# RWKV's transfers through DRAM for the blocks' inverses: part of them issued on ScalarE's queue instead of SyncE's

## The chip, the cores and the metric

The kernel runs on one core of a Trainium2 chip. A core has TensorE (PE) for products, VectorE (DVE), ScalarE (ACT) and GpSimd (POOL) for elementwise work, and SyncE (SP), which here only issues DMA transfers. Each engine works through its own instructions in order; between engines they wait for each other on counters (semaphores). A DMA can be issued from SyncE or from ScalarE; each has a queue of its own. The metric is the device time of one launch in microseconds (us), the median of several runs.

## What is computed

Two layers of a decoder with 256 positions and 1024 channels. In each layer three mixers (retention, forgetting attention and RWKV-7) work side by side on one input projection; their outputs are projected, weighted by gates, added, projected again and added to the input; then comes a SwiGLU feed-forward part. The change lies in RWKV-7, whose state is updated position by position:

```python
def _rwkv7_scan(r, w, k, v, a, b):
    def step(state, inp):
        r_t, w_t, k_t, v_t, a_t, b_t = inp
        sa = jnp.einsum('bhvk,bhk->bhv', state, a_t)
        state = (state * w_t[:, :, None, :] + sa[..., None] * b_t[:, :, None, :]
                 + v_t[..., None] * k_t[:, :, None, :])
        return state, jnp.einsum('bhvk,bhk->bhv', state, r_t)
...
    y = _rwkv7_scan(r_h, hd(decay), k_h, v_h, -kk, kk * a_h)
    y = _head_layernorm(y, RWKV_GN_EPS).reshape(B, S, RWKV_W) * gn_gain
...
    return (y + bonus.reshape(B, S, RWKV_W)) * g

def reference(x, ...):
    for l in range(DEPTH):
        h = _rmsnorm(x, mix_norm[l])
        proj = (h @ w_in[l]).astype(jnp.float32)
...
        merged = (gates[:, :, 0] * (y_ret.astype(x.dtype) @ p_ret[l])
                  + gates[:, :, 1] * (y_fox.astype(x.dtype) @ p_fox[l])
                  + gates[:, :, 2] * (y_rwkv.astype(x.dtype) @ p_rwkv[l]))
        x = x + merged @ w_out[l]
...
```

## The kernel before

**Weights and wide products.** Every product with a weight is done in three parts, high by high, high by low and low by high (L305, L308, L309), to keep float32 accuracy. A weight load of up to 1 MB goes to one of three buffers `raw` (L278, on SyncE's queue). ScalarE rounds a piece of 1024 columns to `whi` (L288), VectorE takes the rest to `wlo` (L289); there are four buffers of each. One piece serves 24 wide products of 128 by 128 by 256. The numbers behind the names (`whi_1935`) are the program's, in the order in which the text makes them.

**RWKV in chunks.** The 256 positions are cut into 4 chunks of 64. For each of the 4 heads and 4 chunks (16 units, handled as 8 pairs of heads) the kernel builds 64 by 64 matrices of the products inside a chunk (`gg`, L810) and needs the inverse of a triangular one. It inverts the four diagonal blocks of 16 by 16 directly and doubles the size twice by products: 16 to 32 (L888 and L895) and 32 to 64 (L907 and L915). The direct inversion is a recurrence of 15 steps on VectorE (L867 multiplies, L869 sums) with one block per partition, while in `gg` a block's rows lie on 16 partitions. So the blocks change their place through DRAM:

1. eight writes from `gg` to `d1` (L820), one for each half h of the partitions and each diagonal block b, 8 KB each;
2. two reads of `d1` to `lt` (L823), the same data for both halves of the columns; GpSimd then sets the diagonals to 1 (L824);
3. the recurrence from `lt` and the unit matrix to `ti`;
4. two writes of `ti` to `d2` (L873), 32 KB each;
5. eight reads of `d2` to the diagonal blocks of `tb` (L878), 8 KB each.

VectorE transposes the two halves of `tb` to `dn` (L883), and TensorE starts the doubling with L888. The results go on through L925 (`pu`), L936 (`par`), L948, L957 to the recurrence over chunks (L967, L972) and the output (L982), then squares (L988), a normalization on VectorE (L990, L394 to L401, L993) and a transposition on TensorE (L1000).

**What sets the order.** RWKV's steps and the wide products are written as generators that take turns by a table of numbers (PACE). What they emit is then put in order for each engine by a scheduler, which goes by priorities and by its own estimate of when each instruction could run. So an edit of the queue that a transfer is issued on can move other instructions too. Each transfer reports its end on one of eight counters (DMAHW0 to DMAHW7), which are taken in turn; a transfer whose counter still belongs to an unfinished one waits for that one first. RWKV's chain runs beside the gates and projections; the products of the third merge (L598 with its wide products) need its result.

Of the kernel before, what the change touches and what calls it, by code (L numbers as in the profile page):

```python
# [24 lines left out]
C = 64  # L25
NC = T // C
B = 32
Q = 16
# [129 lines left out]
class Kernel:  # L158
# [544 lines left out]
    def rwkv(self, l, rw):  # L703
        nc, c = self.nc, self.c
# [96 lines left out]
        gg = big.tile([P, NU, 3 * C], F32, name="gg")  # L801
# [13 lines left out]
        d1 = self.dr.tile([4, 2, NP, Q, Q], F32, name=f"d1_{l}")  # L815
        d2 = self.dr.tile([4, 2, NP, Q, Q], F32, name=f"d2_{l}")
        for h in range(2):
            for b in range(4):
                o = b * Q
                nc.sync.dma_start(d1[b, h].rearrange("u s t -> s u t"), gg[64 * h + o:64 * h + o + Q, h::2, 2 * C + o:2 * C + o + Q])  # L820
        lt = big.tile([P, Q, Q], F32, name="lt")
        for g4 in range(2):
            nc.sync.dma_start(lt[g4 * 64:(g4 + 1) * 64].rearrange("p s t -> p (s t)"), d1.rearrange("b h u s t -> (b h u) (s t)"))  # L823
        nc.gpsimd.memset(lt.rearrange("p s t -> p (s t)")[:, 0:Q * Q:Q + 1], 1.0)  # L824
        ti = big.tile([P, 8, Q], F32, name="ti")
        nc.sync.dma_start(ti, self.dc("tinit"))
# [1 line left out]
        tb = big.tile([P, NP, 2, C], F32, tag="q4", bufs=7, name=self.nm("tb"))  # L828
# [9 lines left out]
        for which in range(2):  # L838
            for a in range(2):
# [6 lines left out]
                else:  # L846
                    mean = sm.tile([P, 2 * NC], F32, tag="mean", bufs=2, name=self.nm("mean"))
                    nc.vector.tensor_reduce(out=mean, in_=ptr, axis=AX.X, op=ALU.add)
                    for h in range(2):
                        nc.scalar.copy(ma[hs[h], a * NC:(a + 1) * NC, C:], ptr[hs[h], h::2, :])  # L850
                        o = hs[1 - h]
# [5 lines left out]
        for p in range(NP):  # L857
            for h in range(2):
                o = hs[1 - h]
# [10 lines left out]
            if i % 6 == 0:  # L870
                yield PACE["rwkv11"]
        for g4 in range(2):
            nc.sync.dma_start(d2.rearrange("b h u c j -> (b h u) c j")[:, g4 * 8:(g4 + 1) * 8, :].rearrange("q c j -> q (c j)"),  # L873
                              ti[g4 * 64:(g4 + 1) * 64].rearrange("p c j -> p (c j)"))
        for h in range(2):
            for b in range(4):
                o = b * Q
                nc.sync.dma_start(tb[64 * h + o:64 * h + o + Q, :, h, o:o + Q], d2[b, h].rearrange("u c j -> c u j"))  # L878
        yield PACE["rwkv12"]

        dn = self.t2.tile([P, NP, C], F32, tag="t2", name=self.nm("dn"))
# [49 lines left out]
        for a in (1, 0):  # L931
            pa = self.ps.tile([P, NC - 1, 2 * C], F32, tag="sm", bufs=SM, name=self.nm("par"))
            for q in range(1, NC):
                for h in range(2):
                    u = unit(a, q, h)
# [8 lines left out]
        for q in range(NC - 1):  # L944
            for a in range(2):
                for h in range(2):
                    u = unit(a, q, h)
# [4 lines left out]
        for q2 in range(NC // 2):  # L952
            for a in range(2):
                for h in range(2):
                    for e in range(2):
                        u = unit(a, 2 * q2 + e, h)
# [19 lines left out]
        for q2 in (1, 0):  # L976
            for a in range(2):
                for e in (1, 0):
                    for h in range(2):
                        q = 2 * q2 + e  # L980
# [267 lines left out]
```

## Time and profile before

| | |
|---|---|
| time, median of 3 runs | 785.89 us (784.91 to 788.56) |
| the profiled execution | 787.26 us, its span 785.5 us |
| SyncE's queue (q1) | 28016 packets, 139.10 MB |
| HBM traffic | 136.97 MB read, 1.33 MB written |
| mean DMA rate | 179 GB/s |
| L888 in layer 0 and layer 1 | from 147.76 and 534.61 us |

Times in rows of the trace are microseconds from the start of the span. A row of the timeline gives the start, the duration, the engine, the line, the operation with output and input, and how often it is repeated; in brackets the idle time of the engine ahead of it and what ended it. "SPq" and "ACTq" are DMA issues of SyncE and ScalarE. Groups give busy time and the mean of one instruction. In the chain of waits each row is one stretch of the chain that ended last, followed back from the end. The ends of products are modelled, and products overlap, so their starts say more than their durations. Layer 0 takes roughly the first half of the span; the places of layer 1 lie 386 to 387 us behind those of layer 0.

### The profile page before, as it was taken

What the parts mean: (1) busy time and instruction counts of PE and PEld (TensorE: products, weight loads), DVE (VectorE), ACT (ScalarE), POOL (GpSimd) and SP (SyncE); (2) the same over time, 40 slices, a digit from 0 to 9 for tenths busy, and PEclk for the clock granted to TensorE, in tenths of its full rate; (3) what the DMA queues carried; (4) which work ended last, traced back from release to release, by engine and by line L of the source; (5) the groups of instructions that cost most, each with busy time, mean ns of one, the idle gap of its engine ahead of it and who ended that gap; (6) DMA issues with size and microseconds to landing.
All of it is one profiled execution on the core that took longest, in us unless ns stands there. A gap on an engine that the chain in (4) does not pass through costs nothing.

```text
span 785.5 us, 16513 instructions
## 1 busy us (share of the span) xinstructions
PE 774.2 (99%) x7002; PEld 754.9 (96%) x7002; DVE 569.7 (73%) x919; ACT 405.0 (52%) x563; POOL 17.8 (2%) x53
## 2 busy tenths in 40 slices
PE   8999999999999999999999999999999999999998
PEld 7999999989999999999998998998999999999997
DVE  5887989968867666656667798987788766666453
ACT  6577545345645454444446774544456544544331
POOL 3100000010000000000020000000000000000000
PEclk9999999999999999999999999999999999999999
DMA  8755434335655555456564554443255455555650
GB/s 325 259 175 183 156 121 164 136 103 198 222 184 195 193 184 214 158 192 201 202 204 178 175 175 162 126 159 138 96 221 194 167 210 204 176 210 172 206 186 28
DMA packets 28234, 140.42 MB, mean 179 GB/s; under 512 B 7648, under 2 KB 9216, under 8 KB 13184
## 3 DMA queue, kind: packets, MB, share of 16 engines
q1 hardware_dynamic: 28016, 139.10, 50.7%
q8 instruction: 55, 0.90, 0.5%
q10 hardware_dynamic: 144, 0.26, 0.1%
q14 instruction: 19, 0.16, 0.1%
HBM read 136.97 MB, written 1.33 MB: 176 GB/s over the span
## 4 chain that ended last, share of the span: by engine, by line
PE 91%; DVE 3%; DMA 2%; ACT 1%; SPq 1%; issue 1%; DVEq 0%; ACTq 0%
PE mm L309 26%; PE mm L305 26%; PE mm L308 26%; DVE wlo L289 1%; DMA d<-ti 1%; PE mqk L488 1%; PE mqk L487 1%; PE mqk L486 1%; DMA raw<-in_win 1%; ACT whi L288 1%; PE mv L488 1%; PE mv L486 1%; PE mv L487 1%; SPq L878 1%; PE pl L1103 1%
## 5 line engine op out<-in xcount | busy, mean ns | idle before, releaser
L288 ACT CAST whi<-raw 128x1024 fp32r<-128x1024 f32 (+1 forms) x257 | 264.8, 1034 | 302.4 <-PE mm L308 214.4
L289 DVE TENSOR_TENSOR wlo<-raw,whi 128x1024 fp32r<-128x1024 f32 (+1 forms) x257 | 308.6, 1203 | 140.0 <-ACT whi L288 139.1
L305 PE MATMUL mm<-xh,whi 128*128 128x256 f32 x1312 | 366.3, 279 | 1.3 <-ACT whi L288 0.9
L308 PE MATMUL mm<-xl,whi 128*128 128x256 f32 x1264 | 351.6, 278 | 0.3 <-DVE xl L442 0.3
L309 PE MATMUL mm<-xh,wlo 128*128 128x256 f32 x1264 | 351.3, 278 | 0.2 <-DVE wlo L289 0.2
L305 PEld LDWEIGHTS mm<-xh,whi 128*128 128x128 f32 x1312 | 246.8, 188 | 2.4 <-ACT whi L288 1.1
L308 PEld LDWEIGHTS mm<-xl,whi 128*128 128x128 f32 x1264 | 237.5, 188 | 1.2 <-issue 0.5
L309 PEld LDWEIGHTS mm<-xh,wlo 128*128 128x128 f32 x1264 | 237.3, 188 | 1.2 <-issue 0.5
L309 PE MATMUL mm<-hi,wlo 128*128 128x256 f32 x576 | 159.7, 277 | 0.0
L308 PE MATMUL mm<-lo,whi 128*128 128x256 f32 x576 | 159.5, 277 | 0.2
L305 PE MATMUL mm<-hi,whi 128*128 128x256 f32 x576 | 159.2, 276 | 0.0
L308 PEld LDWEIGHTS mm<-lo,whi 128*128 128x128 f32 x576 | 108.1, 188 | 0.6 <-DVE lo L426 0.6
L309 PEld LDWEIGHTS mm<-hi,wlo 128*128 128x128 f32 x576 | 108.1, 188 | 0.3
L305 PEld LDWEIGHTS mm<-hi,whi 128*128 128x128 f32 x576 | 108.2, 188 | 0.0
L651 DVE TENSOR_TENSOR h<-t,mm 128x512 f32<-128x512 f32 x22 | 15.1, 687 | 11.5 <-PE mm L309 8.7
L648 DVE TENSOR_TENSOR t<-mm,rstd 128x512 f32<-128x512 f32 (+1 forms) x24 | 15.1, 645 | 8.5 <-PE mm L309 8.5
L486 PE MATMUL mv<-whi,xh 128*128 128x260 f32 (+1 forms) x64 | 18.7, 293 | 0.0
L488 PE MATMUL mv<-whi,xl 128*128 128x260 f32 (+1 forms) x64 | 18.3, 287 | 0.0
L590 ACT ACTIVATE gate<-gate 128x512 f32<-128x512 f32 x24 | 15.1, 629 | 5.6 <-DVE gate L589 5.6
L487 PE MATMUL mv<-wlo,xh 128*128 128x260 f32 (+1 forms) x64 | 18.0, 281 | 0.0
L589 DVE TENSOR_TENSOR gate<-mm,rstd 128x512 f32<-128x512 f32 x24 | 16.4, 684 | 1.0 <-PE mm L309 1.0
L441 ACT ACTIVATE xh<-x,par 128x256 fp32r<-128x256 f32 x32 | 14.8, 501 | 2.5 <-DVE x L662 1.7
(248 smaller groups left out, 685.6 us busy)
## 6 DMA issues: line engine op xcount, KB each, us to landing
raw<-in_wg SPq DMA_DIRECT2D x44, 1024.0 KB
raw<-in_wgate SPq DMA_DIRECT2D x24, 1024.0 KB
raw<-in_wd SPq DMA_DIRECT2D x16, 1024.0 KB
raw<-in_win SPq DMA_DIRECT2D x13, 1024.0 KB
raw<-in_wo SPq DMA_DIRECT2D x8, 1024.0 KB
raw<-in_wd SPq DMA_DIRECT2D x8, 768.0 KB
raw<-in_wqk SPq DMA_DIRECT2D x4, 1024.0 KB
raw<-in_pp SPq DMA_DIRECT2D x4, 1024.0 KB
```

The costliest lines, as they stand in the source:

```text
L288: nc.scalar.copy(hi[:, :m * width], r)
L289: nc.vector.tensor_tensor(out=lo[:, :m * width], in0=r, in1=hi[:, :m * width].bitcast(F32), op=ALU.subtract)
L305: nc.tensor.matmul(out, wh, xh, start=first, stop=False)
L308: nc.tensor.matmul(out, wh, xl, start=False, stop=False)
L309: nc.tensor.matmul(out, wl, xh, start=False, stop=last)
L486: nc.tensor.matmul(out, xh[:, s], wh, start=first, stop=False)
L487: nc.tensor.matmul(out, xh[:, s], wl, start=False, stop=False)
L488: nc.tensor.matmul(out, xl[:, s], wh, start=False, stop=last)
L589: nc.vector.tensor_tensor(out=g, in0=ps, in1=self.b2(rstd), op=ALU.mult)
L590: nc.scalar.activation(g, g, AF.Tanh, scale=0.5)
L648: nc.vector.tensor_tensor(out=t[:, o, :], in0=p, in1=self.bs(rstd, o), op=ALU.mult)
L651: nc.vector.tensor_tensor(out=h, in0=t, in1=pu, op=ALU.mult)
```

## The change

In both layers, the writes of `gg` and the reads into `tb` with h = 1 (four of each eight), both reads of `lt` and both writes of `ti` are issued by ScalarE instead of SyncE: 12 of 20 transfers. What is moved where stays the same.

```diff
         for h in range(2):
             for b in range(4):
                 o = b * Q
-                nc.sync.dma_start(d1[b, h].rearrange("u s t -> s u t"), gg[64 * h + o:64 * h + o + Q, h::2, 2 * C + o:2 * C + o + Q])
+                (nc.sync, nc.scalar)[h].dma_start(d1[b, h].rearrange("u s t -> s u t"), gg[64 * h + o:64 * h + o + Q, h::2, 2 * C + o:2 * C + o + Q])
         lt = big.tile([P, Q, Q], F32, name="lt")
         for g4 in range(2):
-            nc.sync.dma_start(lt[g4 * 64:(g4 + 1) * 64].rearrange("p s t -> p (s t)"), d1.rearrange("b h u s t -> (b h u) (s t)"))
+            nc.scalar.dma_start(lt[g4 * 64:(g4 + 1) * 64].rearrange("p s t -> p (s t)"), d1.rearrange("b h u s t -> (b h u) (s t)"))
...
         for g4 in range(2):
-            nc.sync.dma_start(d2.rearrange("b h u c j -> (b h u) c j")[:, g4 * 8:(g4 + 1) * 8, :].rearrange("q c j -> q (c j)"),
+            nc.scalar.dma_start(d2.rearrange("b h u c j -> (b h u) c j")[:, g4 * 8:(g4 + 1) * 8, :].rearrange("q c j -> q (c j)"),
                               ti[g4 * 64:(g4 + 1) * 64].rearrange("p c j -> p (c j)"))
         for h in range(2):
             for b in range(4):
                 o = b * Q
-                nc.sync.dma_start(tb[64 * h + o:64 * h + o + Q, :, h, o:o + Q], d2[b, h].rearrange("u c j -> c u j"))
+                (nc.sync, nc.scalar)[h].dma_start(tb[64 * h + o:64 * h + o + Q, :, h, o:o + Q], d2[b, h].rearrange("u c j -> c u j"))
```

The scheduler then gives other orders on four engines. On VectorE, at the end of the recurrence in layer 0 (`ttmp` and `ti` are its product and result, `wlo` the splits of weights, `gate` a gate), rows with - are of before, rows with + of the change:

```order
 L867 TENSOR_TENSOR ttmp<-ti,lt 128x8x14
+L869 TENSOR_REDUCE ti<-ttmp 128x8
 L289 TENSOR_TENSOR wlo_1700<-raw_1697,whi_1699 128x1024
-L869 TENSOR_REDUCE ti<-ttmp 128x8
 L867 TENSOR_TENSOR ttmp<-ti,lt 128x8x15
 L869 TENSOR_REDUCE ti<-ttmp 128x8
+L867 TENSOR_TENSOR ttmp<-ti,lt 128x128
 L589 TENSOR_TENSOR gate_1727<-mm_1668,rstd_432 128x512
-L867 TENSOR_TENSOR ttmp<-ti,lt 128x128
+L869 TENSOR_REDUCE ti<-ttmp 128x8
 L289 TENSOR_TENSOR wlo_1813<-raw_1697,whi_1812 128x1024
-L869 TENSOR_REDUCE ti<-ttmp 128x8
```

The last L869, which completes `ti`, stood behind the split `wlo_1813` and now stands ahead of it. A little later VectorE does `wlo_1865`, `gate_1892` and `wlo_1936` as before; the two transposes L883, which stood apart and behind two and three more operations of the merges, now follow `wlo_1936` together.

On ScalarE at the same place (`d_0` is `d2` in layer 0; in brackets what an instruction waits for):

```order
 L862 COPY ma_1350<-pm_1730 128x8x64 [waits PE_49]
+L873 DMA d_0_1330<-ti 64x128 [waits DVE_49]
+L873 DMA d_0_1330<-ti 64x128 [waits DMAHW2_49]
 L288 CAST whi_1864<-raw_1862 128x1024 [waits DMAHW6_49,PE_49,Activation_49]
+L878 DMA tb_1345<-d_0_1330 16x8x16 [waits DMAHW2_49,DMAHW3_49,DMAHW0_49,Pool_49]
+L878 DMA tb_1345<-d_0_1330 16x8x16 x3
 L288 CAST whi_1935<-raw_1862 128x1024 [waits PE_49,Activation_49]
```

Between the casts `whi_1864` and `whi_1935` ScalarE now waits for the two writes of `ti` to land (DMAHW0 and DMAHW2) and issues four reads. The first half that VectorE transposes is the one that these four fill.

On SyncE, from the weight loads ahead of the reading back, with the change:

```order
+L278 DMA raw_1862<-in_pp 128x2048 [waits DMAHW6_49,DMAHW1_49,DVE_49]
+L278 DMA raw_1984<-in_wgate 128x2048 [waits DMAHW7_49,DMAHW4_49,DVE_49]
+L278 DMA raw_2115<-in_wgate 128x2048 [waits DMAHW5_49,DMAHW1_49,DVE_49]
+L878 DMA tb_1345<-d_0_1330 16x8x16 [waits DMAHW2_49,DMAHW0_49,Pool_49]
+L878 DMA tb_1345<-d_0_1330 16x8x16 [waits DMAHW7_49]
+L878 DMA tb_1345<-d_0_1330 16x8x16 [waits DMAHW1_49]
 L878 DMA tb_1345<-d_0_1330 16x8x16
```

The load of `raw_2115` reports on DMAHW1 (the cast of it waits for that counter) and the third read of SyncE's four takes the same counter, so it waits until that load has landed. The writes of `ti` no longer stand behind the load.

On TensorE, where the doubling starts (`mm` are wide products, `pn_257` is L888's output):

```order
 L309 MATMUL mm_1952<-hi_1557,wlo_1700 128x256
 L305 MATMUL mm_1983<-hi_1557,whi_1812 128x256
+L888 MATMUL pn_257_1792<-dn_1789,nn_1347 64x64
 L308 MATMUL mm_1983<-lo_1558,whi_1812 128x256
 L309 MATMUL mm_1983<-hi_1557,wlo_1813 128x256
+L305 MATMUL mm_1983<-hi_1557,whi_1812 128x256
+L308 MATMUL mm_1983<-lo_1558,whi_1812 128x256
+L309 MATMUL mm_1983<-hi_1557,wlo_1813 128x256
+L888 MATMUL pn_257_1792<-dn_1789,nn_1347 64x64 x15
```

L888 stood whole inside `mm_2114`, 122 wide products behind L860. It now begins inside `mm_1983`, 73 wide products behind L860, with one product for the first half, and goes on 5 wide products later. The later steps move forward with it: 19 wide products stand between L895 and L907 in place of 22, and L982 stands in one piece 72 wide products ahead of L1000 in place of 59.

## The prediction, as it was made before the changed kernel was run

> **What bounds the kernel now.** I read the page's busy times and chain first, then what TensorE waits for, then the stretch of layer 0 where the edited transfers stand.
>
> ```profile
> PE 774.2 (99%) x7002; PEld 754.9 (96%) x7002; DVE 569.7 (73%) x919; ACT 405.0 (52%) x563; POOL 17.8 (2%) x53
> PE 91%; DVE 3%; DMA 2%; ACT 1%; SPq 1%; issue 1%; DVEq 0%; ACTq 0%
> ```
>
> TensorE is busy 99% of the span and is 91% of the chain that ended last. The products stay the same in number and shape, so the time can change only by the few places where TensorE's queue stands still. Its waits name one that the edited transfers feed:
>
> ```profile
> PE pn L888 <- DVE dn L883: 1.7, 2, 1.2
> ```
>
> L888 is the first product that uses the inverses read back into `tb`, after VectorE has transposed them to `dn`. Busy time hides part of a stall, since the ends of products are modelled; I therefore take stalls from start to start.
>
> ```profile
> 146.99 0.28 PE L308 MATMUL mm<-lo,whi 128*128 128x256 f32 x1
> 147.76 1.15 PE L888 MATMUL pn<-dn,nn 64*64 64x64 f32 x32 [0.50 <-DVE dn L883]
> ...
> 533.08 0.28 PE L308 MATMUL mm<-lo,whi 128*128 128x256 f32 x1
> 534.61 1.09 PE L888 MATMUL pn<-dn,nn 64*64 64x64 f32 x30 [1.25 <-DVE dn L883]
> ...
> 173.99 0.28 PE L309 MATMUL mm<-xh,wlo 128*128 128x256 f32 x1
> 174.65 0.52 PE L1000 MATMUL pv<-con,ysq 128*128 128x128 f32 x3 [0.39 <-DVE ysq L993]
> ```
>
> Wide products (128x256) start about 0.114 us apart. So L888 costs 147.76 - 146.99 - 0.11 = 0.66 us in layer 0 and 1.42 us in layer 1, and L1000, near the end of RWKV's chain, 0.55 us. This is all that can be won at those places: no edit to transfers can give more than some 5 us of 785.
>
> The chain of waits shows why L888 is late:
>
> ```profile
> 132.14 1.08 PE pm L860 x32
> 133.22 0.32 PE mm L305
> ...
> 136.24 0.49 SPq L873
> 136.78 4.37 DMA d<-ti
> 141.27 0.33 SPq L878
> ...
> 142.60 1.84 DMA tb<-d
> ```
>
> The inverses `ti` are ready at 136.2; writing them takes until 141.2 and reading back until 144.5 for the first half. The issue rows of SyncE show what else its queue holds:
>
> ```profile
> 106.27 4.98 SPq L820 DMA_DIRECT2D d<-gg  x8
> 111.37 0.36 SPq L278 DMA_DIRECT2D raw<-in_wgate  x1
> 112.41 1.14 SPq L823 DMA_DIRECT2D lt<-d  x2
> ...
> 129.57 6.62 SPq L278 DMA_DIRECT2D raw<-in_wgate  x2
> 136.24 1.13 SPq L873 DMA_DIRECT2D d<-ti  x2
> 141.27 3.65 SPq L878 DMA_DIRECT2D tb<-d  x8
> ```
>
> The second of the two weight loads (1 MB each) that begin at 129.57 is issued just before 136.2. The 32 KB writes of `ti` are behind it on the same queue and take 4.4 us, while the `gg` writes with nothing ahead end at 111.25 and have all landed when `lt` is issued at 112.41. That last write began about 0.43 before 111.25, so it took 1.6 us.
>
> **What the edit does to the order.** Counted in the two orders, 122 wide products stand between L860 and L888 before, and 73 now (then one product of L888, 5 wide ones, and the rest of L888). At (146.99 - 133.22)/121 = 0.114 us each TensorE arrives at the first L888 at 133.2 + 73 x 0.114 = **141.5** in place of 147.1. The data must come 5.6 us earlier, or TensorE stands still. I follow the data in layer 0; layer 1 has the same order.
>
> *When `ti` is ready.* VectorE runs the recurrence without gaps to its end:
>
> ```profile
> 134.33 0.37 DVE L867 TENSOR_TENSOR ttmp<-ti,lt 128x128 f32<-128x128 f32 x1
> 134.62 1.21 DVE L289 TENSOR_TENSOR wlo<-raw,whi 128x1024 fp32r<-128x1024 f32 x1
> 135.75 0.28 DVE L869 TENSOR_REDUCE ti<-ttmp 128x8 f32<-128x128 f32 x1
> 137.21 1.23 DVE L289 TENSOR_TENSOR wlo<-raw,whi 128x1024 fp32r<-128x1024 f32 x1 [1.18 <-ACT whi L288]
> 139.94 1.23 DVE L289 TENSOR_TENSOR wlo<-raw,whi 128x1024 fp32r<-128x1024 f32 x1 [0.34 <-ACT whi L288]
> ```
>
> The last split `wlo_1813` (1.21 us) now stands behind the last L869, so `ti` comes at 136.03 - 1.21 = 134.8. The earlier `lt` gives nothing more: VectorE has no gap there to use. The first four `gg` writes on ScalarE (4 x 0.43) and the two reads of `lt` (1.1) fall where ScalarE waits anyway, and the cast that they push back is used several microseconds later; should it be late, 1.9 us is the price.
>
> *Writing `ti`.* Both writes are issued on ScalarE at 134.9 and 135.45. Bounds for the landing are the rows above: 1.6 us (`gg`, nothing ahead) and 4.4 us (`ti` behind a load). The load that was ahead (`raw_2115`) now waits for `wlo_1813` and is issued at 136.1, after them and on another queue. I take 1.8, near the lower row: **137.25**.
>
> [...] The 4.37 us against 1.6 us in this trace says that what is ahead on the queue counts.
>
> *Reading back, ScalarE's half.* ScalarE now waits for that landing with the cast `whi_1935` behind it.
>
> ```profile
> 136.12 1.05 ACT L288 CAST whi<-raw 128x1024 fp32r<-128x1024 f32 x1 [0.57 <-ACT ma L862]
> 138.86 1.05 ACT L288 CAST whi<-raw 128x1024 fp32r<-128x1024 f32 x1 [1.68 <-PE mm L308]
> ...
> 0.73 0.40 ACTq L184 DMA_DIRECT2D raw<-in_win  x1
> ```
>
> One issue took ScalarE 0.40 us at the start of the program, SyncE 3.65/8 = 0.46 here. Four end at 137.3 + 4 x 0.44 = 139.05; the cast, at 138.86 before, starts 0.2 late and ends at 140.1, and `wlo_1936` at 141.4. Its block is used at 146.9, so nothing starves. The transfers land 1.8 us after the last issue began, at 140.4. VectorE then transposes twice, now behind `wlo_1936`: the first `dn` (this half) is ready at 141.45 + 0.71 = **142.2**.
>
> *Reading back, SyncE's half.* Its third read carries a wait for the counter DMAHW1, which `raw_2115` uses: it waits until that load has landed. Before, a load and the small writes behind it took from about 135.9 to 141.2, so under 5.3 us; I take 4.9. Issued at 136.1 it lands at 141.0, the fourth read is issued at 141.5, and lands 1.84 later at 143.35. The second `dn` is ready at **144.1**. Bounds: 142.9, if the load is not waited for, and 144.5 with 5.3 us.
>
> *The sum for L888.* TensorE waits from 141.5 to 142.2 (0.7), runs 5 wide products (0.57) and waits to 144.1 (1.3): **2.0 us** per layer.
>
> *Behind it.* Products and copies of the next steps stand as close as before, with one difference: 19 wide products (2.17 us) in place of 22 between L895 and L907.
>
> ```profile
> L899 DVE TENSOR_TENSOR tb<-tb,pn x4: 673/682/691, 151.3 to 538.8; 64x512 f32<-64x512 f32 x4
> L900 DVE STREAM_TRANSPOSE t<-tb x4: 433/434/440, 152.7 to 540.0; 32x256 f32<-32x256 f32 x4
> ```
>
> VectorE needs 2 x 0.68 + 2 x 0.43 = 2.2 us and some issue time there: 0.25 us of waiting. Later the small steps are spread wider. Now:
>
> ```profile
> 165.64 0.38 PE L309 MATMUL mm<-xh,wlo 128*128 128x256 f32 x1
> 165.95 0.34 PE L982 MATMUL py<-S,ar 64*64 64x64 f32 x8
> 166.23 0.39 PE L305 MATMUL mm<-xh,whi 128*128 128x256 f32 x1
> 166.55 0.34 PE L982 MATMUL py<-S,ar 64*64 64x64 f32 x8
> ```
>
> L982 waits twice 0.2 us (0.31 and 0.32 from start to start instead of 0.11), and each change between wide and small products costs about 0.1. After the edit 24 wide products stand ahead of one unbroken L982: 0.5 us less. Between L982 and L1000 there are 72 wide products in place of 59, 1.5 us more cover, and VectorE no longer has a split between the two L993: the 0.55 us of L1000 goes. Ahead of all this, one L869 is put before a step that L417 waits for:
>
> ```profile
> 119.67 0.28 PE L308 MATMUL mm<-xl,whi 128*128 128x256 f32 x1
> 119.95 0.44 PE L417 MATMUL pvr<-con,ex 128*128 128x128 f32 x2
> ```
>
> There is no cover here (0.28 from start to start), so its 0.2 us counts in full.
>
> **Sum.** After, per layer: 2.0 + 0.25 + 0.2 = 2.45 us of stalls. Before: layer 0 has 0.66 + 0.5 + 0.55 = 1.7, layer 1 1.42 + 0.5 + 0.55 = 2.5. That is +0.75 and 0, together **+0.75 us**. The profiled execution took 787.26 us (span 785.5, 1.8 around it) and would take 788.0; against the median of the runs, 785.89, it gives **786.6 us**. The kernel gives back, in the place it moved L888 to, what earlier data win.
>
> **Rivals.**
>
> *Both halves come in time (faster).* If the load does not hold SyncE's half, the second `dn` is ready at 142.9 and L888 waits 0.85 in all; the sum becomes -1.6: **784.3**. It can't fall to nothing, since `whi_1935` still starts no earlier than 138.86, where TensorE frees its buffer: with `ti` earlier too, L888 waits 0.6, and with L907 and L417 no later than before the sum is -3.0: 782.9. For it: reads of 8 KB that need only 0.46 us each to issue. Against it: the explicit wait for DMAHW1.
>
> *ScalarE's queue is held (slower).* ScalarE stands at its first read-back until `ti` is in DRAM, and behind it in order stand `whi_1935`, `wlo_1936` and both transposes. Each microsecond of the landing beyond 137.25 puts the first `dn` back by one; SyncE's half hides the first 1.2 of them, so it decides from a landing at about 138.4 on. With 4.4 us it lands at 139.8; the reads end at 141.6, the cast at 142.65, the split at 143.9, `dn` at 144.65 and 145.4. L888 waits 3.35, each layer has 3.8 of stalls: +2.1 and +1.3, **789.3**; with `ti` no earlier than today, 2.4 more: 791.7. [...] For it: 4.37 us in the chain. Against it: the load that caused this now comes later.
>
> *The moved transfers change nothing.* The same order on TensorE with data as late as before would cost 5 us a layer, 796; as `ti` itself comes earlier by the order of VectorE, I give it no more than 2 in 100.
>
> **How the numbers follow.** Forecast 0.60, its own range 784.5 to 788.8 (from the bounds of SyncE's half and a landing of 1.6 to 2.6 us); both halves in time 0.17; ScalarE held 0.21; nothing changed 0.02. A measurement of this kernel can tell about 0.5%, 3.9 us, from no change: under 782.0 lies what of the first rival goes beyond its 782.9, 0.07; over 789.8 lies half of the second, the third, and a tail of the forecast, 0.15; the rest, 0.78, is within. The range takes in the first rival's 782.9 and the second's 789.3, with half a microsecond at either end for the terms of 0.2: 782.4 to 789.8.
>
> **What would show it.** L888's wait in layer 0 about 2 us in two pieces, the second longer; the chain with `tb` and the third SyncE read after a weight load landed; `ti` to landing under 2.5 us; L1000 and L982 without waits. Wrong if L888 starts at once (first rival), or if ScalarE's idle time before `whi_1935` grows by over 1.5 us (second).

## The result, and the profile after

The changed kernel takes **791.61 us** (median of 4 runs, 791.37 to 793.10) against 786.0 us before (4 runs), a ratio of 1.0068 [1.0054, 1.0081]. In a second comparison it came to 1.0071 [1.0055, 1.0086]. The forecast was 786.6 (782.4 to 789.8): the kernel is slower by 5.6 us where I had expected hardly any change. The profiled execution took 793.1 us, its span 791.3.

The page's busy times and its chain:

```profile
PE 775.0 (98%) x7002; PEld 756.8 (96%) x7002; DVE 569.0 (72%) x919; ACT 404.3 (51%) x563; POOL 16.0 (2%) x53
...
PE 87%; DVE 7%; DMA 2%; ACT 2%; issue 1%; ACTq 1%; SPq 0%; DVEq 0%
```

And the first line of TensorE's waits (total, how often, the longest):

```profile
PE pn L888 <- DVE dn L883: 6.2, 2, 4.8
```

TensorE has lost 4 points of the chain to the other engines, and one wait at L888 lasts 4.8 us. The timeline of TensorE at L888, in layer 0 and then in layer 1, and at L1000 in layer 0:

```profile
142.64 0.28 PE L305 MATMUL mm<-hi,whi 128*128 128x256 f32 x1
147.74 0.47 PE L888 MATMUL pn<-dn,nn 64*64 64x64 f32 x2 [4.82 <-DVE dn L883]
...
533.79 0.28 PE L305 MATMUL mm<-hi,whi 128*128 128x256 f32 x1
535.45 0.33 PE L888 MATMUL pn<-dn,nn 64*64 64x64 f32 x2 [1.38 <-DVE dn L883]
...
180.83 0.28 PE L309 MATMUL mm<-xh,wlo 128*128 128x256 f32 x1
180.95 0.60 PE L1000 MATMUL pv<-con,ysq 128*128 128x128 f32 x4
```

From start to start L888 now costs 147.74 - 142.64 - 0.11 = 4.99 us in layer 0 (0.66 before) and 1.55 in layer 1 (1.42 before). L1000 waits no more. The two layers run the same instructions in the same order, so something other than the order makes layer 0 different.

A simple account shows where the 5.85 us of span are. I take the last start of L860 in each layer as a mark (133.00 and 519.10 before, 134.21 and 525.36 after). Up to the first mark the changed kernel is 1.2 us later. About 0.7 of it comes from the start of the program, where TensorE stood 1.59 us for a cast and then ran at half clock from 8.6 to 12.0; TensorE's order is still the same there, and the profiled execution of the kernel before has no such stretch. The other 0.5 comes from L417. From mark to mark it takes 391.15 instead of 386.10, **5.05 more**. From the second mark to the end it takes 265.96 instead of 266.37, 0.41 less. Apart from L417, all that the change costs is behind L860 in layer 0; layer 1, forecast at 0, gains a little.

The chain of waits behind L860 in layer 0:

```profile
136.47 0.03 ACTq L873
136.50 0.04 ACT ma L862
136.54 5.69 DMA d<-ti
...
142.38 0.33 ACTq L878
...
144.65 1.05 ACT whi L288
...
146.98 0.72 DVE dn L883
147.70 0.04 issue
147.74 0.47 PE pn L888 x2
```

One write of `ti` needs 5.69 us. In layer 1 the same piece is short:

```profile
527.68 1.93 DMA d<-ti
```

The rest is as drawn in the prediction: ScalarE reads back, casts `whi_1935`, VectorE splits, transposes, and TensorE starts. The DMA issues of ScalarE and SyncE in the timeline, first layer 0, then layer 1:

```profile
136.03 0.47 ACTq L873 DMA_DIRECT2D d<-ti  x1
...
136.54 1.78 ACTq L873 DMA_DIRECT2D d<-ti  x1
...
137.15 0.33 SPq L278 DMA_DIRECT2D raw<-in_wgate  x1
...
527.18 0.46 ACTq L873 DMA_DIRECT2D d<-ti  x1
...
527.68 0.61 ACTq L873 DMA_DIRECT2D d<-ti  x1
...
528.31 0.33 SPq L278 DMA_DIRECT2D raw<-in_wgate  x1
```

In layer 1 both writes have been issued when SyncE issues the load `raw_6916`. In layer 0 the second issue takes 1.78 us, and SyncE issues the load `raw_2115` in the middle of it. What the DMA engines then did is in the view of the DMA queues for three stretches: q1 is SyncE's queue, q10 ScalarE's, q8 the fetching of instructions (packets, MB, share of the 16 engines). The stretches are 136.3 to 138.4, then 138.1 to 141.3, then 141.3 to 142.2:

```profile
q1 hardware_dynamic: 4, 0.03, 13.4%
q10 hardware_dynamic: 80, 0.03, 6.9%
q8 instruction: 1, 0.02, 4.0%
...
q1 hardware_dynamic: 126, 1.02, 84.7%
q10 hardware_dynamic: 3, 0.00, 0.4%
...
q10 hardware_dynamic: 78, 0.03, 12.6%
q1 hardware_dynamic: 18, 0.02, 7.4%
```

While the issue is drawn out, one packet of instructions (16384 bytes, 136.58 to 137.93) is being fetched. The 80 packets are those of the first write. Then 1.02 MB of the load pass, and with them 3 packets of ScalarE's queue; 78 of the second write's 80 packets come only when the load is done. It lands at 142.23.

The last thing to see is the granted clock. The stretches 142 to 148, 148 to 152 and 152 to 160 (engine busy times, then the clock, the DMA share and GB/s):

```profile
142.00:148.00 6.00, 1.18 (x11) 0.98 (x9) 2.22 (x3) 2.51 (x3) 0.00 (x0) 0.76 0.19 21
148.00:152.00 4.00, 4.00 (x40) 3.54 (x40) 2.72 (x4) 0.49 (x1) 0.00 (x0) 0.51 0.64 252
152.00:160.00 8.00, 7.97 (x140) 7.32 (x140) 6.04 (x9) 2.61 (x6) 0.00 (x0) 1.00 0.13 38
```

During the standstill the clock falls to about half (0.51 in 148 to 152) and stays there for 4 us of work. From the first L888 to the first L895 layer 0 takes 4.81 us, layer 1, with the same products at full clock, 3.02: the half clock costs **1.8 us**. Layer 0 then adds up nearly: 4.99 - 0.66 = 4.33 us more at L888, 1.8 for the half clock, 0.2 at L907 and about 1.0 less at L982 and L1000 give 5.3, against the 5.05 from mark to mark.

### The profile page after: what moved, and what is told of

The parts are those of the page before. It is cut to its first block, busy times and chain, and to the rows that moved or that the text cites. A ratio compares the mean times of both kernels' runs of the same rounds, so it can differ in the third digit from the quotient of the medians.

```text
span 791.3 us, 16512 instructions
## 1 busy us (share of the span) xinstructions
PE 775.0 (98%) x7002; PEld 756.8 (96%) x7002; DVE 569.0 (72%) x919; ACT 404.3 (51%) x563; POOL 16.0 (2%) x53
## 4 chain that ended last, share of the span: by engine, by line
PE 87%; DVE 7%; DMA 2%; ACT 2%; issue 1%; ACTq 1%; SPq 0%; DVEq 0%
PE mm L305 25%; PE mm L308 25%; PE mm L309 25%; DVE wlo L289 2%; DVE ttmp L867 1%; DMA d<-ti 1%; PE mqk L488 1%; PE mqk L487 1%; PE mqk L486 1%; DMA raw<-in_win 1%; PE mv L488 1%; PE mv L486 1%; PE mv L487 1%; ACT whi L288 1%; DVE ti L869 1%
## 5 line engine op out<-in xcount | busy, mean ns | idle before, releaser
L598 DVE SCALAR_TENSOR_TENSOR gate<-gate,mm 128x512 f32<-128x512 f32 x24 | 16.1, 678 | 7.5 <-PE mm L309 7.4
```

The costliest lines, as they stand in the source:

```text
L598: nc.vector.scalar_tensor_tensor(out=g, in0=g, scalar=1.0, in1=ps, op0=ALU.add, op1=ALU.mult)
```

## The experiments

Theory A: a fetch of TensorE's instructions draws out the issue of the second write; the load gets ahead of it; small packets wait for a load's packets even from another queue; TensorE stands where the scheduler has put L888, and then runs at half clock. Theory B: the early place of L888 costs by itself. Theory C: ScalarE, held by the reads of `tb`, is the price. Ratios are against the kernel before, on the same chip. "Landing" is the piece of the chain from the last issue of a write of `ti` to its end, "L888" the time from start to start less one product, for layer 0 / layer 1.

| | ratio | landing | L888 |
|---|---|---|---|
| the change, second comparison | 1.0071 [1.0055, 1.0086] | 5.63 / 1.92 | 4.71 / 1.53 |
| fetch moved | 1.0013 [0.9999, 1.0027] | 1.94 / 1.93 | 1.75 / 1.45 |
| one write | 1.0029 [1.0017, 1.0041] | 3.18 / 3.24 | 2.38 / 1.77 |
| first half alone | 1.0012 [0.9999, 1.0026] | 3.01 / 1.89 | 2.62 / 0.91 |
| second half alone | 1.0115 [1.0094, 1.0136] | 4.68 / 4.66 | 4.70 / 4.61 |
| load behind the reads | 0.9992 [0.9976, 1.0008] | 2.48 / 1.92 | 1.63 / 0.87 |
| L888 at 98 | 1.0045 [1.0028, 1.0062] | 5.65 / - | see below |
| load behind, L888 at 90 | 0.9981 [0.9969, 0.9992] | 3.12 / - | 1.06 / none |
| standstill filled | 1.0061 [1.0048, 1.0074] | 5.76 / 1.97 | see below |
| reads all on SyncE | 1.0035 [1.0023, 1.0048] | 5.68 / - | 3.52 / 0.78 |
| before, load behind, L888 at 100 | 0.9946 [0.9929, 0.9962] | 1.90 / - | none |
| load behind, at 90, fetch moved | 0.9960 [0.9946, 0.9974] | 1.93 / - | none |

**The change again.** No edit; it ran on one chip with "load behind the reads", "L888 at 98" and "load behind, L888 at 90".

> The changed kernel as it is, a second time, on one chip with the three that follow. Theory A (a fetch of TensorE's instructions falls on the second write of `ti` in layer 0, so that the weight load gets ahead of it): the same fetch at about 136.5 and the same standstill of 4 to 5 us at L888 in layer 0, 1.5 to 1.8 us in layer 1; ratio to the kernel before 1.005 to 1.008. If the standstill of layer 0 was chance of one execution: 1.5 to 2 us in both layers, ratio 1.001 to 1.003.

Measured: 792.92 us, the second issue 1.40 us, 4.71 us at L888 in layer 0 and 1.53 in layer 1. The standstill is no chance of one execution.

**The fetch moved.** Nothing but TensorE's warm-up at the start differs, by 24 products and as many weight loads more. The changed kernel has 55 fetches in a span of 791.3 us, on average one every 14.4 us and one for 255 of its 14004 products and weight loads; by this average I estimate that 48 instructions more bring each fetch 2.7 us earlier:

```diff
-        for _ in range(22):
-            nc.tensor.matmul(pz, zero[:, 0:P], zero, start=True, stop=True)
+        for n in [T] * 14 + [4] * 32:
+            nc.tensor.matmul(pz[:, 0:n], zero[:, 0:P], zero[:, 0:n], start=True, stop=True)
```

> The changed kernel, with 24 more instruction pairs at the very start of TensorE's program (14 warm-up products of 256 columns and 32 of 4 in place of 22 of 256); no order changes on any engine. [...] Theory A (the fetch draws the issue out, the weight load is then ahead of the write, the landing comes 5.7 us after `ti`, TensorE stands 5.0 us at L888 and then runs at half clock): the second write is issued in about 0.5 us, lands under 2.5 us after `ti`, L888 of layer 0 waits about 2 us like that of layer 1, no half clock behind it; the time is 791.5 - 3.0 - 1.9 = 786.6 us (785 to 788.5). Theory B (L888 stands too early in TensorE's order, and that costs whatever the landing): unchanged in layer 0, 790 to 792. Theory C (ScalarE's queue is held by the reads that it now issues): unchanged, 790 to 792.

Measured: 788.18 us. ScalarE's issues in the timeline of layer 0:

```profile
136.48 0.47 ACTq L873 DMA_DIRECT2D d<-ti  x1
...
136.99 0.61 ACTq L873 DMA_DIRECT2D d<-ti  x1
```

Two pieces of its chain:

```profile
136.99 1.94 DMA d<-ti
...
140.59 3.60 DMA tb<-d
```

And all that its DMA queues show from 136.3 to 138.4, the stretch in which the changed kernel fetched instructions:

```profile
q10 hardware_dynamic: 121, 0.05, 9.3%
```

No packet of instructions passes in this stretch any more. The second issue takes 0.61, the write lands 1.94 behind, ahead of the load, and L888 costs 1.75 instead of 4.7 to 5. B and C, which expected no change, fall. Theory A missed one thing: the half clock did not go (0.83 in the mean of 145 to 155), and the time is 0.2% above the forecast for this run. The row of 3.60 shows what is left: the reads of `tb`, issued behind the load, wait for it, 3.3 to 3.6 us instead of 1.8.

**One write of `ti`** (128 partitions, 64 KB):

```diff
-        for g4 in range(2):
-            nc.scalar.dma_start(d2...[:, g4 * 8:(g4 + 1) * 8, :]..., ti[g4 * 64:(g4 + 1) * 64]...)
+        nc.scalar.dma_start(d2.rearrange("b h u (g c) j -> g (b h u) (c j)", g=2), ti.rearrange("p c j -> p (c j)"))
```

> The changed kernel, with one write of `ti` (128 partitions, 64 KB) in place of two; the order on TensorE stays as with the change (73 wide products, then 5). Theory A: only one issue of about 0.5 us from 136.0 on, which ends before the fetch at 136.6, so nothing slips behind the load: landing about 2 us after `ti` in both layers, L888 waits 1.5 to 2.5 us in each, no half clock, 785 to 788 us. Theories B and C: 790 to 792 us.

Measured: 789.12 us, between the ranges. In layer 0 the issue at 135.28 took 1.07 us; landing takes 3.18 and 3.24 us in the two layers, not 2, though the load is issued 1.1 us behind the start of each write (136.41 and 525.86). So the landing was slower in both layers alike; what made it so was not shown, and the run tests none of the three theories.

**Each half of the change alone.** First the edits of `gg` and `lt`:

```diff
-                nc.sync.dma_start(d1[b, h]...
+                (nc.sync, nc.scalar)[h].dma_start(d1[b, h]...
-            nc.sync.dma_start(lt[g4 * 64:(g4 + 1) * 64]...
+            nc.scalar.dma_start(lt[g4 * 64:(g4 + 1) * 64]...
```

> Only the first half of the change: four of the writes of `gg` and both reads of `lt` on ScalarE, `ti` written and all eight reads of `tb` on SyncE as before. Its order: the writes of `ti` now stand ahead of the load of raw_2115 on SyncE, and 98 wide products stand between L860 and L888 (122 before, 73 with the change), so TensorE comes to L888 at 133.2 + 98 x 0.114 = 144.4. Theory A: with nothing ahead of the writes they land about 1.8 us after `ti` (134.8), at 137; of the eight reads behind the load the last are issued by about 141 and land by 143; `dn` is in time or up to 1 us late: 783 to 786.5 us. Theory B (places that come earlier cost): half of the loss, 788 to 789. Theory C (what holds ScalarE is the reads of `tb`): as before or a little better, 784 to 786.

Measured: 787.66 us, slower than A's and C's ranges and just below B's. The writes of `ti`, now on SyncE ahead of the load, were drawn out too (2.25 us for both issues, 1.13 in the kernel before), and in both layers the second `dn` stands behind a gate and a split on VectorE, which I had not followed. The write landed after 3.01 us in layer 0 although the load was issued behind it, on the same queue: the landing was 1.1 us longer than in layer 1 (1.89), by as much as the issues were drawn out. L888 waits 2.62 and 0.91. In the total this half is neutral.

The second half, the edits of `ti` and `tb`:

```diff
-            nc.sync.dma_start(d2...
+            nc.scalar.dma_start(d2...
-                nc.sync.dma_start(tb[64 * h + o:64 * h + o + Q, :, h, o:o + Q], ...
+                (nc.sync, nc.scalar)[h].dma_start(tb[64 * h + o:64 * h + o + Q, :, h, o:o + Q], ...
```

> Only the second half of the change: both writes of `ti` and four of the reads of `tb` on ScalarE, `gg` and `lt` as before. Its order: the last split wlo_1813 stands ahead of the last L869 again, so `ti` is ready at 136.0 and the load of raw_2115, which waits for that split, is issued on SyncE at about 135.8, just ahead of the writes on ScalarE; 80 wide products stand between L860 and L888, which TensorE reaches at 142.3. Theory A in its wider form (small packets wait behind a load's packets whichever queue they are on): the writes land 4.5 to 6 us after `ti` in both layers, at about 141 to 142, ScalarE is held, L888 waits 4 to 5.5 us in both layers with half clock behind it: 793 to 798 us. Theory A in its narrow form (only the drawn-out issue did it): landing 1.8, at 138, L888 waits about 2 us, 786 to 788. Theory C: both layers as layer 0 of the change, 793 to 796, even if the landing is early.

Measured: 796.66 us. SyncE's and ScalarE's issues in the timeline of layer 0:

```profile
135.85 0.33 SPq L278 DMA_DIRECT2D raw<-in_wgate  x1
...
136.05 1.15 ACTq L873 DMA_DIRECT2D d<-ti  x2
```

And the piece of its chain behind them:

```profile
136.59 4.68 DMA d<-ti
```

Nothing is drawn out here (two issues in 1.15). The load is issued 0.2 ahead, on another queue, and the landing takes 4.7 us in both layers, about what it took in the kernel before behind a load on the same queue (4.37). So in these runs what mattered was which of the two is issued first, not on which queue. A drawn-out issue by itself added what it is longer by, 1.1 to 1.2 us (landings of 3.01 and 3.12 us in the table, with no load ahead, against 1.9); the rest up to 5.7 comes with the load that it lets ahead. In the changed kernel's profile 128 rows of 8192 bytes make up the load (138.11 to 141.34), and 126 packets of its queue passed with 3 of ScalarE's (138.1 to 141.3).

**The load behind the reads.** An order edge (it fixes the order in which the scheduler places two instructions, and nothing is waited for) puts `raw_2115` and `raw_6916` behind SyncE's last read of `tb`:

```diff
+            tc.add_manual_dep(k.loads[19 + 65 * l].ins, k.rd[8 * l + 3].ins.name,
+                              mybir.DependencyInfo(mybir.DependencyClass.NoSync, mybir.DependencyReason.DATA), reason="order")
```

> The changed kernel, with the load of raw_2115 (raw_6916 in layer 1) put behind SyncE's four reads of `tb` on its queue, so that no load is issued between `ti` and the reads; 78 wide products ahead of L888 in one piece. Theory A, second part (the small packets wait for the packets of a load whichever queue they are on): even with a drawn-out issue the writes land 2 to 3 us after `ti` in both layers, and the reads 1.8 us after the last issue in place of 3.3; L888 waits 0.3 to 1.2 us in both layers, with little or no half clock behind it; 784 to 786.5 us, ratio 0.997 to 1.000. If the slow landing in layer 0 comes from the drawn-out issue alone: layer 0 waits over 3 us still, ratio 1.004 or more. If holding ScalarE's casts behind the reads is what costs (theory C): 1.5 us or more in both layers, ratio 1.001 to 1.003.

Measured: 786.23 us, 6.7 us below the change on the same chip. The timeline of layer 0, SyncE and then TensorE:

```profile
138.64 2.03 SPq L878 DMA_DIRECT2D tb<-d  x4
140.79 2.62 SPq L278 DMA_DIRECT2D raw<-in_wgate  x2
...
144.44 0.74 PE L888 MATMUL pn<-dn,nn 64*64 64x64 f32 x18 [1.47 <-DVE dn L883]
```

And its chain:

```profile
136.00 2.48 DMA d<-ti
...
139.89 2.08 DMA tb<-d
```

The second issue is drawn out here too (1.17 us), and yet the write lands after 2.48 us and the reads after 2.08; no load lies between. No half clock follows (1.00 in 145 to 155). Layer 0 waits a little more than I expected, 1.63, of which 0.6 is the longer issue.

**L888 later.** The change as it is, with the same kind of edge from L888 to the 98th wide product behind L860 (`k.wide[769 + 2832 * l]`):

> The changed kernel, with L888 held back on TensorE until 98 wide products have been issued behind L860 (73 with the change), 2.85 us later; queues and loads as with the change. Theory A with the place as its second factor (a late landing costs only what the place leaves uncovered): layer 1 waits 0 at L888 in place of 1.6; layer 0 waits 2.1 us if its landing is late again, 0 if not; 784.5 to 788 us, ratio 0.999 to 1.003. If RWKV's chain behind L888 has no slack, what is won at L888 is lost behind it (L936, L967, L1000): ratio 1.004 or more.

Measured: 790.45 us, a miss. Layer 1 has the late place's gain (0.35 us of waiting). In layer 0 the landing was late again (5.65), and TensorE stood 3.6 us, but ahead of L888. Rows of ScalarE and TensorE:

```profile
143.71 1.05 ACT L288 CAST whi<-raw 128x1024 fp32r<-128x1024 f32 x1 [5.36 <-PE mm L309]
...
148.22 0.36 PE L305 MATMUL mm<-hi,whi 128*128 128x256 f32 x1 [3.44 <-DVE gate L598]
```

ScalarE can't cast `whi_1935` before its reads are issued, so VectorE's split, the transposes and a gate behind them are late, and a wide product waits for the bank that this gate frees. A later place of L888 only moves the wait to another product, since ScalarE's queue carries the lateness on.

**Reads all on SyncE** tests C directly (`nc.sync` for all eight reads, the rest as with the change; 98 products):

> The changed kernel, with all eight reads of `tb` on SyncE: ScalarE still writes `ti` but its casts no longer stand behind the reads. 98 wide products ahead of L888, as in the experiment that held it there. Theory A: the second write meets the same fetch, lands 5 to 6 us after `ti` in layer 0; SyncE's eight reads go behind the load, the third one waits until it has landed, and eight issues take 3.7 us; `dn` no earlier than 147 to 148 in layer 0, 2.5 to 3.5 us of waiting at L888 in layer 0 and 1 to 3 in layer 1: ratio 1.003 to 1.007. Theory C (ScalarE held by the reads is the price): the wide products no longer starve for casts and splits, ratio 1.002 or less.

Measured: 789.98 us. Landing 5.68 in layer 0 as A says, 3.52 us at L888. With ScalarE free of the reads TensorE waits at L888 instead of ahead of it, for as long; the ratio is 0.1% below that of the run with ScalarE's reads, less than either interval. C is not the price.

**Both edges**, load behind the reads and L888 behind 90 products:

> Both: the load behind SyncE's reads, and L888 held until 90 wide products have been issued. Theory A: nothing to wait for at L888 in either layer (0 to 0.3 us), full clock all through; against the kernel before, its 0.66 and 1.42 us at L888, and the waits at L982 and L1000 (about 1 us a layer) are gone: 782.5 to 785 us, ratio 0.995 to 0.998, faster than both kernels. If the place or ScalarE's reads cost in another way: not below 1.000.

Measured: 785.82 us, 0.8 above my range but faster than both kernels. Layer 1 waits nowhere at L888, layer 0 still 1.06, with the second issue drawn out to 1.80 us. With the warm-up of the moved fetch in addition:

> The load behind SyncE's reads and L888 behind 90 wide products, with TensorE's instruction fetches moved by 24 instruction pairs at the start: the second write of `ti` is then issued in 0.5 to 0.65 us in layer 0 too (1.3 with the fetch on it), `dn` is 0.7 us earlier, the 1.06 us that layer 0 waited at L888 fall to 0.3 or less: 784.5 to 785.5 us, ratio 0.996 to 0.998. If the fetch has no part in it: 0.998 to 0.999 as without the shift.

Measured: 783.44 us, 1.1 below my range, L888 without a wait in both layers, the issues 0.47 and 0.62.

**The standstill filled.** To see the half clock's part, 38 products of zeros in layer 0 ahead of L888, in its own tile:

```diff
+        self.fil += [nc.tensor.matmul(px[:, 0:4, :]..., self.zero[:, 0:P], self.zero, start=True, stop=True) for _ in range(38 if l == 0 else 0)]
```

> The changed kernel, in layer 0 alone with 38 products of zeros (128x256, into the tile that L888 then overwrites) behind the 73 wide products: TensorE is busy for 4.3 us of the 5 that it waits at L888. If the half clock that the profile shows from 145.1 to 152.0 comes from the standstill, it goes, and the 16 pairs of L888 and the products behind them start 0.051 and 0.114 us apart in place of 0.10 and 0.21: 1.5 to 2 us less than the changed kernel, 790.5 us, ratio 1.0045 to 1.0055 (changed: 1.007). If the half clock has another cause or costs nothing: 1.007.

Measured: 791.72 us, unclear by the total. By stage it is clear. The stretch 145 to 155 of the changed kernel (the clock is the third number from the right):

```profile
145.00:155.00 10.00, 7.26 (x86) 6.60 (x87) 6.85 (x9) 2.74 (x4) 0.00 (x0) 0.66 0.32 108
```

And of this one:

```profile
145.00:155.00 10.00, 8.93 (x159) 7.82 (x159) 8.81 (x13) 3.20 (x5) 0.00 (x0) 1.00 0.29 107
```

Full clock, and 389.47 us from mark to mark instead of 391.15. But in layer 1 SyncE's four reads took 4.84 us to issue in place of 4.46, and the chain's piece behind the last of ScalarE's reads 3.79 in place of 3.41; whether a fetch moved by the 76 instructions more did it was not shown. L888 cost 1.96 there, a lower clock followed (0.57 in 533 to 537), and from the second mark to the end it took 268.01 us, 2.05 more than the changed kernel.

**Without ScalarE's queue.** The kernel before, all 20 transfers on SyncE, with the load behind the eight reads and L888 behind 100 products:

```diff
+            tc.add_manual_dep(k.loads[19 + 65 * l].ins, k.rd[8 * l + 7].ins.name, ...)
+            for i in k.dbl[16 * l:16 * l + 16]:
+                tc.add_manual_dep(i.ins, k.wide[771 + 2832 * l].ins.name, ...)
```

> The kernel before, all 20 transfers on SyncE, with the load of raw_2115 (raw_6916) put behind the eight reads of `tb` and L888 held until 100 wide products have been issued: does the load's place alone do it, without ScalarE's queue? The writes of `ti` (ready at 136.0) have no load ahead: landing at 139 in place of 141.2; eight reads are issued by 142.8 and land by 144.6; `dn` is ready at 145.3 to 146.5, L888 is reached at 144.6 and waits 0.7 to 1.9 us in both layers; 785 to 787.5 us, ratio 0.998 to 1.001. If the queue matters by itself: above 1.003.

Measured: **782.52 us**, the fastest of all and 2.5 us below the range that I expected. SyncE's issues and TensorE at L888 in layer 0:

```profile
135.05 1.13 SPq L873 DMA_DIRECT2D d<-ti  x2
137.56 3.64 SPq L878 DMA_DIRECT2D tb<-d  x8
141.31 0.85 SPq L278 DMA_DIRECT2D raw<-in_wgate  x2
...
143.69 1.15 PE L888 MATMUL pn<-dn,nn 64*64 64x64 f32 x32
```

Landing 1.90, nothing drawn out, no wait at L888 in either layer, clock 1.0. From mark to mark it takes 384.28 us, 1.82 less than the kernel before, and behind the second mark 2.34 less. With the kernel before, the second half alone and the fetch moved, this gives all four cases of the landing: on one queue 4.37 us with the load issued ahead and 1.90 without, on two queues 4.68 and 1.94. Which of the two edges gives how much of the time was not tried apart.

## Why the prediction was wrong

**The step that failed** is "Writing `ti`": "The load that was ahead (`raw_2115`) now waits for `wlo_1813` and is issued at 136.1, after them and on another queue. I take 1.8, near the lower row: 137.25". In layer 1 exactly this happened: the landing is at 529.61, 2.46 us behind `ti` (527.15), where the prediction has 137.25 - 134.8 = 2.45. In both layers the load is issued only 0.6 us behind the start of the second write (137.15 - 136.54 and 528.31 - 527.68). I counted this order as safe, and in layer 0 a drawn-out issue of 1.78 us undid it: the load's packets went first, and the write landed 5.69 us behind its issue where the sum has 1.8. Put the measured landing (142.23 - 136.00 = 6.23 us behind `ti`) into my own working for the second rival: `dn` at 145.9 and 146.6, 4.5 us of waiting at L888, measured 4.99. So the path of that rival is what happened in layer 0, and the term that the forecast had wrong is the landing. I had taken the 4.37 against 1.6 us of the trace before as proof that what is ahead on the same queue decides; the second half alone, with the load ahead on the other queue, landed after 4.68.

**Not foreseen:** the half clock behind a standstill, 1.8 us. The second rival had no term for it either. That its outer figure, 791.7, lies beside the measured time is luck: it has both layers late and `ti` no earlier than before, and neither came about.

**Right in mechanism:** ScalarE is held and `whi_1935`, `wlo_1936` and `dn` are pushed back one for one (its idle time before `whi_1935` grew from 1.68 to 5.16, the sign that I had named for the second rival). L888 in a layer without the slip: forecast 2.0, measured 1.55 (the two halves of `dn` come closer together than I had them: SyncE's half 9.2 us behind `ti`, forecast 9.3, but ScalarE's 8.25, forecast 7.4, since its reads wait for the load's packets). L907: forecast 0.25, measured 0.19 and 0.23. L982 and L1000: gone, as forecast (no wait at L1000, and 0.21 from start to start at an unbroken L982). L417: forecast 0.2, measured 0.5 in layer 0. Layer 1 as a whole: forecast 0, measured -0.41 behind its mark.

**In the chances:** the rival that came out had 0.21, and the range ended at 789.8, since I let the case of a held queue end at the 4.4 us of one row. Both of its terms, the landing (5.69 us) and what TensorE does after a standstill (1.8 us at half clock), came out larger than any row of the kernel before shows.

## What to carry to other kernels

A small transfer on which an engine waits should be issued before a large one, with margin; in these runs another queue didn't free it from the large one (landing 4.68 us behind a load on the other queue, 4.37 on the same). Where a scheduler moves a consumer up by 5 us because the data should come earlier, ask by how little the data's chain is ahead of the next large load, and what a microsecond of jitter in one DMA issue does to that order. Holding one load back by one order edge took the changed kernel from 1.0071 to 0.9992; the kernel before with such an edge and one that puts L888 behind 100 products, and no second queue, was the fastest of all at 0.9946.

## What the runs showed of the hardware

The issue of a small transfer was drawn out in most of the places where it met a fetch of TensorE's instructions. In the traces of the two kernels six issues of L820, L873 and L878 met one: four took 1.56 to 1.97 us, two 0.43 and 0.44. These fetches are single packets of 16384 bytes, 55 of them in the span, one for about 255 of TensorE's instructions (7002 products and as many weight loads). That they are TensorE's is inferred from this count and from the moved fetch: with 24 products more in TensorE's warm-up none passed from 136.3 to 138.4, where the changed kernel has one (136.58 to 137.93). In the changed kernel the second write takes 1.78 us with the fetch on it and, with the fetch moved, 0.61. Without a fetch on it no issue of L820, L873 or L878 took over 0.66 us in the traces of the two kernels. The issues of the weight loads (L278) were not drawn out: 16 of them met a fetch in the changed kernel, and each took 0.33 us. What makes this difference was not tried. The kernel before has two such places among the transfers that the change is about, an issue of L820 at 108.14 with 1.70 us (fetch 108.07 to 109.44) and one of L878 at 530.03 with 1.97 (fetch 530.21 to 531.61). The second stands on the chain of layer 1, right ahead of the landing, `dn` and L888: it is 1.5 us longer than the issues before it (0.43), and L888 waits 1.42 us there. The changed kernel's list of TensorE's waits names no fetch, but the queue that issued a transfer at that moment was held, as the 1.78 us show. The drawn-out issues of the other experiments (1.07 to 1.80 us for one) have no fetch shown beside them; that one stood there too is my inference from these two traces.

A lower clock followed the standstills of 3.5 to 5.0 us each time (0.66 to 0.83 in stretches of 10 us from their end or middle on), and also those of 1.75 (fetch moved, 0.83), 1.96 (standstill filled, layer 1, 0.83) and 2.38 us (one write, 0.66), but not one of 2.62 (first half, 1.00) nor those of 1.4 to 1.8 us in layer 1 (1.00 in 520 to 545). So the length alone doesn't decide it, and what else does was not shown. In the trace of the changed kernel the clock is at half from 8.59 to 12.00, at the end of the standstill of 1.59 us there, and from 145.12 to 151.95, from the middle of the standstill at L888 on. Whether a standstill of 2 to 3 us was paid for twice can't be told here from its length.
